# A quarter of the gate and up contraction by Strassen's seven block products, in a two-layer decoder trunk on one core

## The chip, the cores and the metric

The kernel runs on one core of one Trainium2 chip. The metric is the device time of one execution in microseconds (us); before the change it is 2117.68 us, the median of three runs (2116.63 to 2117.85 us).

## The reference

Two layers act on 256 tokens of width 2048. The first mixes by a diagonal state space (S5) and a gated projection, the second by causal attention. Each then has a SwiGLU of inner width 5632, which holds most of the arithmetic:

```python
D_MODEL = 2048; SEQ = 256; D_FF = 5632

def swiglu(u, w_gate, w_up, w_down):
    return (jax.nn.silu(u @ w_gate) * (u @ w_up)) @ w_down

for i in range(DEPTH):                       # DEPTH = 2
    ...                                      # mixer of layer i
    u = rmsnorm(h, g_ffn[i])
    h = h + swiglu(u, w_gate[i], w_up[i], w_down[i])
return rmsnorm(h, g_final)
```

Everything is float32 at the interface.

## The kernel before, in words

Every weight matrix is cut into tiles of 512 rows by 512 columns (1 MB). Such a tile is one job. All 344 jobs stand in one list, and `run_stream` goes through it: matmuls of job i, then the preparation of job i+2 (`split_upto`), then whatever functions were pended behind job i. The order on each engine is the order in which these calls are written; no scheduler changes it.

Preparing a job: SyncE loads the tile into `raw` (three buffers); ScalarE rounds it to `hi` (L98) and VectorE forms `lo = raw - hi` (L99), each in two halves of 128x1024. `hi` and `lo` have two buffers each, so job i+2 can be rounded when job i's matmuls have let go. In the first seven jobs GpSimd forms `lo`. The activations are split in the same way, so a product is three matmuls: hi by hi, lo by hi, hi by lo (`mm3`, L108 to L110). A job of the kind used here is 4 blocks of 128 rows x 2 token halves x 3 = 24 matmuls with 512 columns.

In the SwiGLU the inner width is 11 chunks of 512 columns: 6 in the first half of the stage, 5 in the second, each half followed by its part of the down projection. A chunk is 4 gate jobs and 4 up jobs (the input width 2048 is 4 tiles of 512 rows). Each job adds into two PSUM banks, one per token half. Chunks alternate between the four `acc` banks and the `x` and `tr` banks. ScalarE takes silu of the gate banks (L686), VectorE multiplies by the up banks (L693), and two jobs into the next chunk TensorE transposes the product row by row (L701), ScalarE and VectorE splitting it into `g` (L704, L705).

The activations `u_f` are transposed from `h` by `hT_blocks`: four blocks of 128 features per call of `u_chunk`, TensorE (L141), ScalarE (L145), VectorE (L146). For the first SwiGLU these calls stand among the last jobs of the gated projection (there GpSimd adds bias and residual, L597 and L611, and VectorE multiplies, L609); for the second among the last jobs of the output projection of the attention (`w_o`).

Of the kernel before, what the change touches and what calls it, by code (L numbers as in the profile page):

```python
# [30 lines left out]
def trunk_kernel(ctx: ExitStack, tc: tile.TileContext, par, x_tok, x_grp, b_st, g_st, c_st, cst, gvec,  # L31
# [57 lines left out]
    def split_upto(n):
        while st["split"] < min(n, len(jobs)):  # L90
            i = st["split"]
            load_upto(i + 3)
# [8 lines left out]

    def mm3(psums, opnd, kb0, j, first, last, kbs=range(4), halves=range(2)):
        for kb in kbs:
            for a in halves:
# [2 lines left out]
                pr = psums[a]
                pe.matmul(pr, oh, j.hi[:, kb], start=first and kb == 0, stop=False)  # L108
                pe.matmul(pr, ol, j.hi[:, kb], start=False, stop=False)  # L109
                pe.matmul(pr, oh, j.lo[:, kb], start=False, stop=last and kb == 3)  # L110
# [24 lines left out]
    def hT_blocks(blocks, dst, g, base=0):  # L135
        for b0 in range(0, len(blocks), 2):
# [5 lines left out]
            for bb in range(2):  # L142
# [510 lines left out]
    def g_at(l, hf, kb):  # L653
        n, b = divmod(kb, 8)
        if (l, hf, n) not in G:
            G[l, hf, n] = big.tile([128, 2, 8, L], F32R, name=f"g{l}{hf}{n}", tag="ABC"[n])
# [527 lines left out]
```

## Time and profile before

| | |
|---|---|
| median of three runs | 2117.68 us |
| the profiled execution | 2113.61 us, span 2111.8 us |
| TensorE matmuls busy | 2082.5 us, 99% |
| VectorE busy | 1135.2 us, 54% |
| ScalarE busy | 905.6 us, 43% |
| GpSimd busy | 150.1 us, 7% |
| read from HBM | 370 MB, 176 GB/s over the span |

The span is what the trace covers; the profiled execution's own time is 1.8 us more. Busy time of matmuls counts overlapping ones once. In the tables of groups, the busy time and mean of a matmul include the time in which the next one already runs.

### The profile page before, as it was taken

To read this page: it belongs to the slowest core of one execution; us is meant where nothing else is said; L and a number is where in the kernel's file an instruction comes from. 1 tells how busy PE (TensorE), PEld (TensorE's weight loads), DVE (VectorE), ACT (ScalarE), POOL (GpSimd) and SP (SyncE) were. 2 spreads that over 40 slices of the span, in tenths; PEclk is the share of its full clock that TensorE was granted. 3 is DMA by queue.
4 is the path that set the end of the run, shared out by engine and by line. 5 is a ranking of instruction groups with operands and counts; after the bars stand their busy time and mean duration, and the time that the engine had idled before them with its cause. 6 is when DMAs were issued, how large, how long until landed. Compare 5 with 4: busy or idle time off the path is not lost.

```text
span 2111.8 us, 27975 instructions
## 1 busy us (share of the span) xinstructions
PE 2082.5 (99%) x11712; PEld 1754.9 (83%) x11712; DVE 1135.2 (54%) x1661; ACT 905.6 (43%) x1161; POOL 150.1 (7%) x105
## 2 busy tenths in 40 slices
PE   7999999999999999999999999999999999999998
PEld 6778788888888888889999998888888888888886
DVE  8984854444444445455555455554444544445454
ACT  6344544434334344444444444454444333443443
POOL 7741400000000000000000000000000000000000
PEclk9999999999999999999999999999999999999999
DMA  3035555555555555555545544555555555555554
GB/s 140 25 126 157 197 190 188 197 183 197 182 197 199 181 197 180 198 180 180 180 160 180 172 167 160 181 193 184 185 194 193 186 199 190 189 192 186 195 194 149
DMA packets 54046, 376.14 MB, mean 178 GB/s; under 512 B 6432, under 2 KB 6944, under 8 KB 9120
## 3 DMA queue, kind: packets, MB, share of 16 engines
q1 hardware_dynamic: 53920, 374.36, 51.5%
q8 instruction: 91, 1.49, 0.3%
q14 instruction: 35, 0.29, 0.0%
HBM read 370.14 MB, written 2.10 MB: 176 GB/s over the span
## 4 chain that ended last, share of the span: by engine, by line
PE 95%; DVE 3%; ACT 1%; issue 1%; DMA 0%; SPq 0%; ACTq 0%; POOLq 0%; POOL 0%
PE acc L109 18%; PE acc L110 18%; PE acc L108 18%; PE x L110 4%; PE x L108 4%; PE x L109 4%; PE tr L109 4%; PE tr L108 4%; PE tr L110 4%; PE acc L793 3%; PE acc L792 3%; PE acc L791 3%; PE x L464 1%; PE tr L141 1%; PE acc L273 1%
## 5 line engine op out<-in xcount | busy, mean ns | idle before, releaser
L99 DVE TENSOR_TENSOR lo<-raw,hi 128x1024 fp32r<-128x1024 f32 x674 | 805.9, 1237 | 674.5 <-ACT hi L98 674.4
L98 ACT ACTIVATE hi<-raw 128x1024 fp32r<-128x1024 f32 x688 | 690.4, 1052 | 715.4 <-PE acc L109 413.3
L108 PE MATMUL acc<-hi,g 128*128 128x512 f32 x704 | 274.9, 390 | 0.0
L110 PE MATMUL acc<-lo,g 128*128 128x512 f32 x704 | 274.0, 389 | 0.0
L109 PE MATMUL acc<-hi,g 128*128 128x512 f32 x704 | 274.0, 389 | 0.0
L108 PE MATMUL acc<-hi,u_f 128*128 128x512 f32 x640 | 251.1, 392 | 1.1 <-ACT hi L98 1.0
L110 PE MATMUL acc<-lo,u_f 128*128 128x512 f32 x640 | 249.5, 390 | 1.1 <-DVE lo L99 1.1
L109 PE MATMUL acc<-hi,u_f 128*128 128x512 f32 x640 | 249.3, 390 | 0.0
L110 PEld LDWEIGHTS acc<-lo,g 128*128 128x128 f32 x704 | 132.2, 188 | 27.6
L109 PEld LDWEIGHTS acc<-hi,g 128*128 128x128 f32 x704 | 132.2, 188 | 27.1
L108 PEld LDWEIGHTS acc<-hi,g 128*128 128x128 f32 x704 | 132.2, 188 | 27.1
L108 PE MATMUL x<-hi,u_f 128*128 128x512 f32 x384 | 151.3, 394 | 0.0
L110 PE MATMUL x<-lo,u_f 128*128 128x512 f32 x384 | 149.7, 390 | 0.0
L109 PE MATMUL x<-hi,u_f 128*128 128x512 f32 x384 | 149.5, 389 | 0.0
L108 PE MATMUL tr<-hi,u_f 128*128 128x512 f32 x384 | 149.4, 389 | 0.0
L109 PE MATMUL tr<-hi,u_f 128*128 128x512 f32 x384 | 149.4, 389 | 0.0
L110 PE MATMUL tr<-lo,u_f 128*128 128x512 f32 x384 | 149.4, 389 | 0.0
L110 PEld LDWEIGHTS acc<-lo,u_f 128*128 128x128 f32 x640 | 120.1, 188 | 26.9 <-DVE lo L99 1.9
L108 PEld LDWEIGHTS acc<-hi,u_f 128*128 128x128 f32 x640 | 120.2, 188 | 26.4 <-ACT hi L98 1.9
L109 PEld LDWEIGHTS acc<-hi,u_f 128*128 128x128 f32 x640 | 120.2, 188 | 24.8 <-DVE u_f L146 0.3
L110 PEld LDWEIGHTS x<-lo,u_f 128*128 128x128 f32 x384 | 72.1, 188 | 15.2
L108 PEld LDWEIGHTS tr<-hi,u_f 128*128 128x128 f32 x384 | 72.1, 188 | 15.0
(238 smaller groups left out, 2865.1 us busy)
## 6 DMA issues: line engine op xcount, KB each, us to landing
raw<-w_gate SPq DMA_DIRECT2D x88, 1024.0 KB, 4.8
raw<-w_up SPq DMA_DIRECT2D x88, 1024.0 KB, 4.8
raw<-w_down SPq DMA_DIRECT2D x88, 1024.0 KB, 4.8
raw<-w_kv SPq DMA_DIRECT2D x32, 1024.0 KB, 4.8
raw<-w_glu SPq DMA_DIRECT2D x16, 1024.0 KB, 4.9
raw<-w_q SPq DMA_DIRECT2D x16, 1024.0 KB, 4.8
raw<-w_o SPq DMA_DIRECT2D x16, 1024.0 KB, 4.8
h<-x_tok SPq DMA_DIRECT2D x2, 1024.0 KB, 7.8
```

What stands on the lines that cost most here:

```text
L98: act.activation(j.hi[:, s], j.raw[:, s], AF.Copy)
L99: (pool if i < NPRE else dve).tensor_tensor(j.lo[:, s], j.raw[:, s], j.hi[:, s], op=OP.subtract)
L108: pe.matmul(pr, oh, j.hi[:, kb], start=first and kb == 0, stop=False)
L109: pe.matmul(pr, ol, j.hi[:, kb], start=False, stop=False)
L110: pe.matmul(pr, oh, j.lo[:, kb], start=False, stop=last and kb == 3)
L141: pe.transpose(tr[:, bb, a], h[:, a, 128 * b:128 * b + 128], ident)
L273: pe.matmul(wbk[:, 0:w], ident, cs[:, 0:w], start=True, stop=True)
L464: pe.matmul(yb[64 * g2:64 * g2 + 64, g], H[q][r, ri, gl + g2].rearrange("p k c -> p (k c)"), Z[r, :, ri, 2 * (8 * o + g) + b], start=ri == ...
L791: pe.matmul(p, j.hi[:, kb, s], u[:, 0], start=first and kb == 0 and n % 2 == 0, stop=False)
L792: pe.matmul(p, j.hi[:, kb, s], u[:, 1], start=False, stop=False)
L793: pe.matmul(p, j.lo[:, kb, s], u[:, 0], start=False, stop=last and kb == 3 and n % 2 == 1)
```

## The change

For 10 of the 11 chunks of each layer (all but chunk 0) the first tile of 512 rows of gate and up is no longer two jobs of 24 matmuls. With the activations as a 2x2 matrix of blocks (token half x 256 rows) and the weights as another (256 rows x gate or up), the product is formed with seven block products instead of eight (`s_add`, `mm1`: 6 matmuls each). The weight sums are four additions of 128x1024 on VectorE per chunk (`S_T1` to `S_T4`, L769); the two tiles are loaded into buffers of their own (`s_load`); products 1 to 7 are jobs of one half unit each, rounded like the others. The activation sums are made once per layer in `s_combine`, which takes the place of the first `hT_blocks`. Some products stand in two or more of the four results. They are added by reading the PSUM bank between products into a row (`s_evac`) and correcting the results with it after the last job. The other three tiles of gate and up (`X` jobs) add into the same banks, partly between the products. `hi` and `lo` become two fixed buffers used half by half; the pool of rows goes from 5 to 9 buffers; the transposed result of chunk c goes to banks of chunk c itself.

```diff
-    rows = ctx.enter_context(tc.tile_pool(name="rows", bufs=5))
+    rows = ctx.enter_context(tc.tile_pool(name="rows", bufs=9))
...
+            if j.make is not None:
+                j.make()
+            for p in range(units(j)):
+                raw = j.raw[:, 2 * p:2 * p + 2] if j.part is None else j.part()
+                u = st["unit"]
+                st["unit"] += 1
+                hi, lo = [t[:, 2 * (u % 2):2 * (u % 2) + 2] for t in parts[u // 2 % 2]]
+                act.activation(hi, raw, AF.Copy)
+                (pool if i < NPRE else dve).tensor_tensor(lo, raw, hi, op=OP.subtract)
...
+    def split_ahead(i):
+        split_upto(i + 2)
+        n = units(jobs[i + 1]) if i + 1 < len(jobs) else 3
+        k = i + 2
+        while k < len(jobs) and n + units(jobs[k]) <= 3:
+            n += units(jobs[k])
+            k += 1
+        split_upto(k)
...
+    def mm1(pr, opnd, j, first, join):
+        for kb in range(2):
+            oh, ol = opnd(0, kb), opnd(1, kb)
+            pe.matmul(pr, oh, j.hi[kb], start=first and kb == 0, stop=False, skip_group_check=join)
+            pe.matmul(pr, ol, j.hi[kb], start=False, stop=False, skip_group_check=join)
+            pe.matmul(pr, oh, j.lo[kb], start=False, stop=first and kb == 1, skip_group_check=join)
...
+    def s_combine(un, g):
...
+        for b in range(2):
...
+            for bb in range(2):
+                k = b + 2 * bb
+                x = X[:, bb].rearrange("p a t -> p (a t)")
+                act.activation(X[:, bb], tr[:, bb], AF.Copy, scale=g[:, k:k + 1])
+                act.activation(uT[un][:, 0, k], x, AF.Copy)
+                dve.tensor_tensor(uT[un][:, 1, k], x, uT[un][:, 0, k], op=OP.subtract)
+            dve.tensor_tensor(V[:, 2], X[:, 0, 1], X[:, 0, 0], op=OP.subtract)
+            dve.tensor_tensor(V[:, 0], X[:, 0, 1], X[:, 1, 1], op=OP.subtract)
+            dve.tensor_tensor(V[:, 1], X[:, 1, 1], V[:, 2], op=OP.subtract)
+            dve.tensor_tensor(V[:, 3], X[:, 1, 0], V[:, 1], op=OP.subtract)
+            act.activation(SC["c"][:, 0, :, b], V, AF.Copy)
+            dve.tensor_tensor(SC["c"][:, 1, :, b], V, SC["c"][:, 0, :, b], op=OP.subtract)
...
+            for t, w in (("F", wu), ("E", wg)):
+                nc.sync.dma_start(T[t], w[4 * c].rearrange("p (k n) -> p k n", k=4))
...
+            if n == 0:
+                gr[c, 0] = row()
+                act.activation(P(), acc["gate"][0], AF.Copy)
+            if n == 1:
+                T["u"] = row()
+                tt(T["u"], acc["up"][0], P(), OP.subtract)
+            if n == 2:
+                tt(T["u"], acc["up"][1], T["u"], OP.add)
+            if n == 4:
+                gr[c, 1] = row()
+                tt(v(), acc["up"][0], P(), OP.subtract)
+            if n == 9:
+                T["s"] = row()
+                act.activation(T["s"], acc["gate"][0], AF.Silu, scale=r[:, 0:1])
+                tt(T["u"], acc["gate"][1], T["u"], OP.subtract)
+                act.activation(T["u"], T["u"], AF.Silu, scale=r[:, 1:2])
+            if n == 12:
+                tt(P(), acc["up"][0], P(), OP.subtract)
+                tt(P(), P(), T["s"], OP.mult)
+                tt(v(), acc["up"][1], v(), OP.add)
+                tt(v(), v(), T["u"], OP.mult)
+                gu_end()
...
+                    pend.append((j0 - 5, s_load(l, c, wg, wu)))
+                    pend.append((j0 - 3, S_T1))
+                    pend.append((j0 - 2, S_T2))
+                    pend.append((j0 - 2, S_T3))
+                    for i in (1, 6, 7):
+                        s_add(i, un, own)
+                    X("gate", wg, 1)
+                    s_add(5, un, own)
+                    X("gate", wg, 2)
+                    for i in (2, 3, 4):
+                        s_add(i, un, own)
+                    X("gate", wg, 3)
+                    for kg in (1, 2, 3):
+                        X("up", wu, kg)
+                    for n in (0, 1, 2, 4, 9, 12):
+                        pend.append((j0 + n, s_evac(n, c, r)))
```

So a changed chunk is 13 jobs: products 1, 6, 7 (P1, P6, P7), gate tile 1 (X1), P5, gate tile 2 (X2), P2, P3, P4, gate tile 3 (X3), up tiles 1 to 3 (U1 to U3).

How instructions now stand, at three places. First TensorE at the start of chunk 1, where before the first job of a chunk goes to both gate banks (`x`) in turn, three matmuls each; before:

```order
L108 MATMUL x_3145<-hi_3173,u_f_2665 128x512
L109 MATMUL x_3145<-hi_3173,u_f_2665 128x512
L110 MATMUL x_3145<-lo_3174,u_f_2665 128x512
L108 MATMUL x_3146<-hi_3173,u_f_2665 128x512
L109 MATMUL x_3146<-hi_3173,u_f_2665 128x512
L110 MATMUL x_3146<-lo_3174,u_f_2665 128x512
```

and of the change, the end of P1, the start of P6, the start of P7, and the transposes of chunk 0 behind it (`sc` holds the activation sums):

```order
L144 MATMUL x_3126<-lo_1488,u_f_2641 128x512
L142 MATMUL tr_3138<-hi_1487,sc_u_f_2642 128x512
L143 MATMUL tr_3138<-hi_1487,sc_u_f_2642 128x512
L144 MATMUL tr_3138<-lo_1488,sc_u_f_2642 128x512
...
L142 MATMUL tr_3139<-hi_1495,sc_u_f_2642 128x512
...
L849 MATMUL acc_137_3162<-cs,row_3031 128x128 x4
```

A product stays in one bank for six matmuls and takes a new `hi` and `lo` half; over the whole program TensorE has 120 rows fewer (9231 for 9351).

Second, ScalarE at the start of a chunk. Before, the gate banks of the old chunk have long been read, and roundings of whole tiles follow one another up to the copy of the transposed rows:

```order
L98 ACTIVATE hi_3734<-raw_3666 128x1024 x2
L98 ACTIVATE hi_3768<-raw_3698 128x1024 x2
L704 ACTIVATE g_3779<-acc_149_3774 128x4x128
L98 ACTIVATE hi_3808<-raw_3732 128x1024 x2
L704 ACTIVATE g_3779<-acc_150_3814 128x4x128
```

Of the change, at the start of chunk 3 (`st` and `su` are weight sums, the L808 row is the reading of P1 from its bank, `raw_3675` is X1):

```order
L111 ACTIVATE hi_1495<-st_3_3553 128x1024
L111 ACTIVATE hi_1487<-su_3_3552 128x1024
L808 ACTIVATE row_3693<-x_3685 128x512
L111 ACTIVATE hi_1487<-raw_3675 128x1024
L111 ACTIVATE hi_1495<-raw_3675 128x1024
L111 ACTIVATE hi_1495<-st_3_3553 128x1024
L852 ACTIVATE g_3724<-acc_157_3719 128x4x128
```

The rounding of X1 now stands behind a reading that waits for P1's last matmul.

Third, VectorE near the end of the gated projection, where `u_f` of the first SwiGLU is begun. Before:

```order
L609 TENSOR_TENSOR row_2615<-row_2615,zk 128x8x32 x2
L609 TENSOR_TENSOR row_2616<-row_2616,zk 128x8x32 x2
L146 SCALAR_TENSOR_TENSOR u_f_2665<-tr_2666,gv,u_f_2665 128x256 x2
L146 SCALAR_TENSOR_TENSOR u_f_2665<-tr_2675,gv,u_f_2665 128x256 x2
L99 TENSOR_TENSOR lo_2711<-raw_2603,hi_2710 128x1024 x2
```

Of the change (the six rows of `X_u_f_2663` that follow, alike, are left out):

```order
L672 TENSOR_TENSOR row_2594<-row_2594,zk 128x8x32 x2
L201 TENSOR_TENSOR u_f_2641<-X_u_f_2644,u_f_2641 128x256 x2
L202 TENSOR_TENSOR V_u_f_2645<-X_u_f_2644 128x128
L203 TENSOR_TENSOR V_u_f_2645<-X_u_f_2644 128x128
L204 TENSOR_TENSOR V_u_f_2645<-X_u_f_2644,V_u_f_2645 128x128
L205 TENSOR_TENSOR V_u_f_2645<-X_u_f_2644,V_u_f_2645 128x128
L207 TENSOR_TENSOR sc_u_f_2642<-V_u_f_2645,sc_u_f_2642 128x4x128
...
L112 TENSOR_TENSOR lo_1488<-raw_2583,hi_1487 128x1024 x2
```

The rounding of the second-last job of the projection stands behind 14 operations of VectorE where there were 4, and on ScalarE, in the same place, behind 10 where there were 4.

## Rows read from the trace of the kernel before

**Rows 1.** The page: busy time and share of each engine.

```profile
PE 2082.5 (99%) x11712; PEld 1754.9 (83%) x11712; DVE 1135.2 (54%) x1661; ACT 905.6 (43%) x1161; POOL 150.1 (7%) x105
```

**Rows 2.** Windows: busy of each engine, TensorE's clock, DMA share, GB/s.

```profile
1600.00:1700.00 100.00, 100.00 (x450) 82.84 (x449) 48.81 (x46) 39.28 (x42) 0.00 (x0) 1.00 0.55 189
222.00:265.00 43.00, 40.81 (x190) 32.29 (x188) 35.71 (x45) 23.83 (x42) 16.96 (x12) 1.00 0.50 175
```

**Rows 3.** Timeline of TensorE, 1640 to 1653 us: start, duration.

```profile
1640.87 0.39 PE L108 MATMUL acc<-hi,g 128*128 128x512 f32 x1
...
1650.85 0.39 PE L110 MATMUL acc<-lo,g 128*128 128x512 f32 x1
...
1651.76 0.60 PE L701 MATMUL x<-cs,row 128*128 128x128 f32 x4
...
1652.43 0.39 PE L109 MATMUL acc<-hi,g 128*128 128x512 f32 x1
```

**Rows 4.** Groups by shape, 1400 to 2000 us: busy, mean ns | idle before.

```profile
L99 DVE TENSOR_TENSOR lo<-raw,hi 128x1024 fp32r<-128x1024 f32 x217 | 256.2, 1222 | 252.1 <-ACT hi L98 252.1
L693 DVE TENSOR_TENSOR row<-tr,row 128x512 f32<-128x512 f32 x12 | 7.7, 681 | 0.0
...
L98 ACT ACTIVATE hi<-raw 128x1024 fp32r<-128x1024 f32 x217 | 218.1, 1052 | 284.4 <-PE acc L109 164.3 <-PE tr L109 75.4 <-PE x L109 44.6
L704 ACT ACTIVATE g<-acc 128x512 fp32r<-128x512 f32 x10 | 6.0, 598 | 37.6 <-PE acc L701 37.6
```

**Rows 5.** Groups by shape, whole run: smaller operations of both engines.

```profile
L236 DVE TENSOR_TENSOR gam<-gam,T 128x256 f32<-128x256 f32 x1 | 0.4, 419 | 0.0
L224 DVE TENSOR_TENSOR gam<-gam 128x64 f32<-128x64 f32 x1 | 0.2, 218 | 0.0
...
L133 ACT ACTIVATE jk<-h 128x512 f32<-128x512 f32 x30 | 18.8, 626 | 25.0 <-DVE h L727 15.0 <-DVE h L722 8.3 <-POOL h L611 1.6
L499 ACT ACTIVATE zT<-tr 128x256 fp32r<-128x256 f32 x16 | 4.8, 388 | 7.1 <-PE tr L494 7.1
```

**Rows 6.** Timeline: ScalarE's start behind TensorE, VectorE's behind ScalarE.

```profile
1640.85 2.01 ACT L98 ACTIVATE hi<-raw 128x1024 fp32r<-128x1024 f32 x2 [3.43 <-PE tr L109]
...
1641.94 2.36 DVE L99 TENSOR_TENSOR lo<-raw,hi 128x1024 fp32r<-128x1024 f32 x2 [3.08 <-ACT hi L98]
```

**Rows 7.** Timelines of four engines at the end of the gated projection.

```profile
225.32 0.47 ACT L145 ACTIVATE u_f<-tr,gv 128x256 fp32r<-128x256 f32 x1 [1.37 <-PE tr L141]
...
229.03 2.00 ACT L98 ACTIVATE hi<-raw 128x1024 fp32r<-128x1024 f32 x2
...
220.31 4.06 DVE L99 TENSOR_TENSOR lo<-raw,hi 128x1024 fp32r<-128x1024 f32 x2
...
230.11 2.36 DVE L99 TENSOR_TENSOR lo<-raw,hi 128x1024 fp32r<-128x1024 f32 x2 [0.47 <-ACT hi L98]
...
219.76 3.53 POOL L597 TENSOR_TENSOR row<-row,row 128x512 f32<-128x512 f32 x2 [1.76 <-DVE row L596]
...
226.95 1.29 POOL L611 TENSOR_TENSOR h<-h,row 128x512 f32<-128x512 f32 x1 [0.43 <-DVE row L609]
...
231.03 0.39 PE L108 MATMUL acc<-hi,zT 128*128 128x512 f32 x1
...
231.48 0.41 PE L110 MATMUL acc<-lo,zT 128*128 128x512 f32 x1
...
243.52 0.50 PE L108 MATMUL acc<-hi,u_f 128*128 128x512 f32 x1 [0.51 <-ACT hi L98]
```

**Rows 8.** Timelines at the attention's output projection, ScalarE and TensorE.

```profile
1333.92 0.47 ACT L145 ACTIVATE u_f<-tr,gv 128x256 fp32r<-128x256 f32 x1 [0.63 <-PE tr L141]
...
1336.73 2.00 ACT L98 ACTIVATE hi<-raw 128x1024 fp32r<-128x1024 f32 x2
...
1340.43 0.48 PE L108 MATMUL acc<-hi,o 128*128 128x512 f32 x1
```

**Rows 9.** The page, DMA issues: KB each, us from issue to landing.

```profile
raw<-w_gate SPq DMA_DIRECT2D x88, 1024.0 KB, 4.8
```

More of the change, by code (lines that the diff above doesn't have):

```diff
@@ L106, in mm3 @@
                 ol = opnd(1, kb0 + kb, a)
[L107 to L110, printed above, removed]
+                pr, jn = psums[a], a in joins
+                pe.matmul(pr, oh, j.hi[kb], start=first and kb == 0 and not jn, stop=False, skip_group_check=jn)
+                pe.matmul(pr, ol, j.hi[kb], start=False, stop=False, skip_group_check=jn)
+                pe.matmul(pr, oh, j.lo[kb], start=False, stop=last and kb == 3 and not jn, skip_group_check=jn)
+    def mm1(pr, opnd, j, first, join):
[4 more added lines that the diff above has]
+            pe.matmul(pr, oh, j.lo[kb], start=False, stop=first and kb == 1, skip_group_check=join)
     def run_stream(i0, i1):
@@ L578, in f @@
                 u_tile(name)
-            hT_blocks(range(4 * c, 4 * c + 4), uT[name], gv[:, gs])
+            if c == 0 and name != "u_kv":
+                s_combine(name, gv[:, gs])
+            else:
+                hT_blocks(range(4 * c, 4 * c + 4), uT[name], gv[:, gs])
         pend.append((j, f))
@@ L655, in g_at @@
         if (l, hf, n) not in G:
[L656 removed]
+            G[l, hf, n] = big.tile([128, 2, 8, L], F32R, name=f"g{l}{hf}{n}", tag=("ABC", "BCD")[l][n])
         return G[l, hf, n], b
@@ L669, in gu_acc, with gu_end, gu_job @@
             new_acc(nm)
+            CT[nm] = last_tags()
         else:
             acc[nm] = [bank("x" if nm == "gate" else "tr") for _ in range(2)]
-    def gu_job(nm, un, own, kg):
+            CT[nm] = ["x" if nm == "gate" else "tr"] * 2
+    def gu_end():
+        NT[:] = [CT["gate"][0], CT["up"][1]]
+    def gu_job(nm, un, own, kg, first, last, joins=None):
         o = opnd1(lambda: uT[un])
         def f(j):
-            if kg == 0:
+            if joins is None and first:
                 gu_acc(nm, own)
-            mm3(acc[nm], o, 4 * kg, j, kg == 0, kg == 3)
+            mm3(acc[nm], o, 4 * kg, j, first, last, joins=joins or ())
+        return f
@@ L694, in up_evac, with g_rows @@
         return f
-    def g_rows(l, hf, c, own, a):
+    def g_rows(l, hf, c, src, a):
         def f():
-            t = sil[c][a]
-            tr = bank(own if own else "x").rearrange("p (b t) -> p b t", b=4)
+            t = src()
+            tr = bank(NT[a]).rearrange("p (b t) -> p b t", b=4)
             for b in range(4):
```

107 lines of the change are left out of this document (83 added, 24 removed).

## Prediction

> **What bounds the kernel now.** I read the page first. TensorE is busy 99% of the span, VectorE 54%, ScalarE 43% [rows 1]. A busy TensorE need not be at its peak, so the windows come next: in a stretch inside the SwiGLU TensorE is busy 100.00 of 100 us at granted clock 1.00 (its upper level, 2.4 GHz), VectorE 48.8, ScalarE 39.3, GpSimd 0, DMA 0.55 [rows 2]. The timeline of that stretch shows matmuls at a fixed pace: from 1640.87 to 1650.85 us there are 44 intervals, 0.2268 us each [rows 3]. The 0.39 us of one matmul overlaps the next; the price of a matmul with 512 columns is 0.2268 us. Other engines wait there: VectorE for ScalarE (252 us in 600), ScalarE for TensorE (284 us) [rows 4]. So in the SwiGLU a matmul less is time less, as long as VectorE and ScalarE stay ahead.
>
> One place is different. At the end of the gated projection VectorE is busy 35.7 of 43 us, and TensorE waits: the first gate matmul starts at 243.52 behind the rounding by ScalarE [rows 2, 7]. There the chain through VectorE and ScalarE sets the end, and the change puts work into that chain.
>
> **What is removed.** Per changed chunk 48 matmuls become 7 x 6 = 42. 10 chunks in 2 layers: 120 matmuls, the 120 rows that TensorE has fewer. 120 x 0.2268 = 27.2 us [rows 3]. The Trainium skill (TensorE: Matmul & The Clock Gate, section "Wait — 56ns, not 53.3ns?") gives columns / 2.4 GHz + 2.5 ns from start to start, 215.7 ns at 512 columns; by it the term would be 25.9 us. The row has 226.8 ns, and I use the row.
>
> **What a changed chunk asks of VectorE and ScalarE.** TensorE's time: 186 matmuls x 0.2268 = 42.2 us, and two groups of transposes, each 0.45 us (1651.76 to 1652.43 less one interval) [rows 3]: 43.1 us. VectorE: 19 roundings for 16 and 4 weight sums, which have the shape and both operands in SBUF like L99: 23 x 1.22 = 28.1; 8 operations of 512 columns in `s_evac` and 2 of `g_rows` at 0.68: 6.8 [rows 4]. Sum 34.9 of 43.1 us (before: 16 x 1.22 + 4 x 0.68 = 22.2 of 44.4). ScalarE: 19 x 1.05 + some 5 x 0.65 = 23 us. All lie under TensorE as totals, so what counts is where TensorE waits for one late item. I followed the orders of a chunk with these durations and 0.04 us between engines (1640.85 + 1.05 to 1641.94) [rows 6].
>
> The tightest place is X1 at the start of a chunk. On ScalarE the reading of P1 (0.60, as L704) stands ahead of X1's rounding [rows 4]. P1's last matmul ends 0.39 - 0.23 = 0.16 us into P6. Then 0.04 + 0.60, + 1.05 for `hi`, + 0.04 + 1.22 for `lo`, + 0.05 until TensorE: 3.2 us. TensorE gets to X1's third matmul, the first that needs `lo`, after P6 and P7 (12 x 0.2268 = 2.72), one group of transposes (0.45) and two matmuls (0.45): 3.6 us. Slack 0.45 us. VectorE is free by then: its four operations on the old chunk end 0.16 + 4 x 0.68 = 2.9 us after that chunk's last matmul, and `hi` of X1 comes 1.36 (P1) + 0.16 + 0.64 + 1.05 = 3.2 us after it. The other places have more. P4, behind the sum `S_T4`, which stands behind the reading of P5: from P5's end VectorE still has P2's `lo` (1.7 with its `hi`), then 0.68 + 1.22 + 1.22, then ScalarE 1.05 and `lo` 1.22, 7.1 us in all; TensorE has X2, P2, P3 and two matmuls, 8.6 us. At U2, VectorE waits for X3's end to read a gate bank, with U2's rounding queued behind; U2 is needed one job (5.44 us) later. Nothing here waits, so I cost the products, sums and readings at nothing; the cover is 0.45 us per chunk at the least, and each 0.1 us beyond it would cost 20 x 0.1 = 2 us.
>
> Readings between products also hold back TensorE's next write to the bank: P1's bank is written again by X1, 3.2 us later, when the reading has taken 0.8; P6's by P5, P5's by P3, each with a job of 5.44 us between. No wait.
>
> **Transfers.** Bytes are the same; two tiles go to buffers of their own. They are issued when P3 and `S_T4` let go, some 6 us before X3, and are needed by `S_T1` about two jobs later, 15 us after issue, against 4.8 us to land one and a DMA share of 0.55 [rows 2, 9]. In SyncE's queue U3's tile stands behind them; it waits for X3's rounding anyway. No cost.
>
> **What is added once per layer: `s_combine`.** On ScalarE one of its two halves is: scale, round, scale, round (0.47 and 0.39 twice, 1.7 us, as in [rows 5, 7]), then VectorE's second `lo` (0.42) and four sums of 128 columns, between the 0.22 of 64 and the 0.42 of 256 columns, with two dependent pairs (1.2 us together), then the rounding of 512 columns (0.63) [rows 5]. That is 4.0 us, and the second half stands behind the first on ScalarE: 8.0 us until ScalarE can round the next weight tile.
>
> First SwiGLU: before, ScalarE starts at 225.32 and rounds the next tile at 229.03, 3.7 us later [rows 7]. Now 8.0: 4.3 us late. That tile's job starts at 231.03, and its third matmul came a trace late already (0.41 us for 0.39, at 231.48) [rows 7]: no slack. The chain from there to 243.52 is VectorE's and ScalarE's, where TensorE waits even now, so the delay isn't made up: + 4.3 us.
>
> Second SwiGLU: before, 1333.92 to 1336.73 [rows 8]. Now the rounding starts at 1341.9, `hi` is there at 1343.0, `lo` at 1344.3. The job started at 1340.43 [rows 8] and would need `lo` 0.54 us later: + 3.3 us. The next `u_chunk` and rounding then come late too, by 0.3 us beyond the delayed job: + 3.6 us. Bounds for both layers: if the sums go at 0.22 us and the operations overlap at the seams, a half is 3.5 us and the cost 3.3 + 2.6 = 5.9 us; if the sums take 0.42 us each, a half is 4.5 us and the cost 9.9. I take 7.9, near the middle, since 128 columns lie between the two rows.
>
> **Sum.** - 27.2 + 7.9 = - 19.3 us. The profiled execution is 2113.6 us (span 2111.8 + 1.8), which would become 2094.3. The median of the three runs lies 4.1 us above it; the same difference gives 2117.7 - 19.3 = **2098.4 us**, 0.9% less.
>
> **The rivals.**
> 1. `s_combine` is hidden: TensorE has work queued, or the later stalls before the SwiGLU shrink by what is lost ahead of them. Then 27.2 less at most 3: 2090.5 to 2093.5. Against it: TensorE waits there already [rows 7].
> 2. The start of a chunk waits. If reading P1 or rounding X1 comes 0.5 us beyond the slack, 20 x 0.5 = 10 us: 2108. For it: 0.45 us is thin, and ScalarE has a waiting instruction ahead of X1. Against it: the rows of the long operations vary little.
> 3. GpSimd slows `s_combine`. While GpSimd adds (219.76 to 223.3) VectorE's two roundings take 4.06 us instead of 2.36 [rows 7]; the replaced L146 reads PSUM and was not slowed. GpSimd's next addition, 226.95 for 1.29 us, lies on the first operations of `s_combine`, which read two operands from SBUF: up to 1.3 us more, 2099.7. The Trainium skill (SBUF — State Buffer, section "Who interferes with whom") says of two such operations that the second blocks until the first ends; by that rule the whole 1.29 us is added.
> 4. The other side: VectorE becomes the bound in the chunks. With d for an operation of 1024 columns its work is 23 d + 6.8; it fills 43.1 us at d = 1.58 us, and at 1.62 us (1 us over, in 20 chunks) the gain of 19.3 is gone; with 1.7 us, 20 x 2.8 = 56 us: 2154. For it: 2.03 us is what L99 takes beside GpSimd [rows 7]. Against it: GpSimd has no instruction in the SwiGLU [rows 2], and 1.22 is the mean of 217 [rows 4].
> 5. The seven products aren't cheaper: six matmuls in a row into one bank, or a wait for a half at each, at 0.26 us instead of 0.2268 for 840 matmuls, + 28 us: no change. Against it: three in a row into one bank show no longer interval [rows 3].
>
> **How the numbers follow.** Forecast 0.55 (2094 to 2103 with the bounds of `s_combine` and some tenths per chunk); rival 1 0.12; rival 2 0.15; rival 3 0.10; rival 4 0.04; rival 5 0.04. Range 2091 to 2107: rival 1 nearly whole, the forecast, rival 3, half of rival 2. A measurement of this kernel tells 0.2% (4.2 us) from no change. Faster: all but rivals 4 and 5 and the far end of 2: 0.90; same 0.05; slower 0.05.
>
> **What would show it.** Right: TensorE's matmuls of 512 columns 120 fewer at the same 0.227 us; in the 20 chunks no row of TensorE that waits for X1's `lo` or `hi`; the first gate matmul not at 243.5 but about 4 us later, and gaps of about 3 us in all at the 11th of the 16 jobs of `w_o`; VectorE at some 80% in the chunks. Wrong: gaps in front of X1 or P4 in every chunk; a mean of L112 over 1.3 us there; a longer interval inside a product; or no delay at `s_combine`.

## The result: 2097.6 us, 1.0% faster, and the profile after

The changed kernel takes 2097.62 us (median of 4 runs, 2094.18 to 2098.23) against 2117.76 us of the kernel before on the same chip (4 runs, 2116.63 to 2118.51): a ratio of 0.9902, 95% interval 0.9885 to 0.9919. The forecast was 2098.4 us. The execution that was profiled took 2097.13 us, with a span of 2095.3 us (before: 2113.6 and 2111.8).

Line numbers below are those of the changed kernel: `mm3` is L135 to L137 and `mm1` L142 to L144 (third matmul, the one that needs `lo`: L137, L144), the rounding of a weight tile is L111 (`hi`) and L112 (`lo`), `s_combine` L195 to L207, the plain path for the activations L175 to L180, a weight sum L769, the reading of P1 L808.

First the page's line of busy times; it answers to [rows 1].

```profile
PE 2061.8 (98%) x11592; PEld 1736.3 (83%) x11592; DVE 1387.9 (66%) x1941; ACT 1000.5 (48%) x1253; POOL 149.9 (7%) x105
```

TensorE has 120 matmuls fewer, VectorE 280 instructions more. TensorE still fills the span. The windows show what the busy share hides (window, its length, busy time of PE, PEld, DVE, ACT and POOL with counts, TensorE's clock, DMA share, GB/s): one stretch in the chunks, and the two places where TensorE had waited for `s_combine`.

```profile
236.00:240.00 4.00, 2.97 (x7) 2.12 (x8) 3.75 (x6) 4.00 (x8) 0.47 (x1) 0.65 0.16 25
1336.00:1340.00 4.00, 3.62 (x9) 2.91 (x10) 2.91 (x6) 1.91 (x6) 0.00 (x0) 0.57 0.40 100
1500.00:1600.00 100.00, 100.00 (x454) 82.85 (x453) 78.64 (x80) 51.72 (x58) 0.00 (x0) 1.00 0.51 180
```

In the chunks TensorE is busy 100.00 of 100 us at clock 1.00, with VectorE at 78.6 where it was at 48.8 [rows 2]. At the other two places the clock was down to 0.65 and 0.57, which no window of before shows. The groups of 1400 to 2000 us answer to [rows 4]: one rounding on VectorE still takes 1223 ns, so more work on that engine did not make it slower.

```profile
L112 DVE TENSOR_TENSOR lo<-raw,hi 128x1024 fp32r<-128x1024 f32 x182 | 217.7, 1223 | 97.0 <-ACT hi L111 95.0
L111 ACT ACTIVATE hi<-raw 128x1024 fp32r<-128x1024 f32 x183 | 189.9, 1056 | 113.2 <-PE acc L136 78.5 <-PE tr L136 19.0 <-PE x L136 5.4
```

TensorE's list of waits over the whole run names the two places, and of 300 to 1250 us and 1385 to 2080 us it has no entry at all: no chunk waits (us in total, times, longest).

```profile
PE acc L135 <- ACT hi L111: 5.8, 3, 3.7
...
PE acc L137 <- DVE lo L112: 1.6, 3, 0.5
```

The account is made with instructions that stand at the same point of both programs. First in the trace of before (start, duration), then after: a matmul behind the transposes that feed `uT` (gated projection, then attention output projection), and the first matmul of the second SwiGLU.

```profile
225.79 0.39 PE L109 MATMUL acc<-hi,zT 128*128 128x512 f32 x1
...
1334.39 0.39 PE L109 MATMUL acc<-hi,o 128*128 128x512 f32 x1
...
1373.18 0.39 PE L108 MATMUL acc<-hi,u_f 128*128 128x512 f32 x1
```

```profile
227.45 0.39 PE L136 MATMUL acc<-hi,zT 128*128 128x512 f32 x1
...
1327.11 0.39 PE L136 MATMUL acc<-hi,o 128*128 128x512 f32 x1
...
1370.26 0.39 PE L135 MATMUL acc<-hi,u_f 128*128 128x512 f32 x1
```

- Up to the first marker: 227.45 - 225.79 = + 1.66 us. Nothing there was changed: the first matmul of the state-space part (L397, before L337) comes at 25.13 instead of 23.44 us. Over the profiled executions of all kernels here it lies between 23.3 and 27.7 us, and one kernel (the filled waits, below) has it at 23.90 in one execution and at 26.30 in another. It is the spread between executions.
- From the first marker to the matmul that follows the last wait in chunk 0 (265.37 us before, 271.71 after): 44.26 us for 39.58, + 4.68.
- From the second marker to the second SwiGLU: 43.15 us (1370.26 - 1327.11) for 38.79, + 4.36.
- The rest: from the end of chunk 0's waits to the second marker 1055.40 us for 1069.02, from the second SwiGLU's first matmul to the end of the span 725.04 for 738.62, - 13.62 and - 13.58 us, where 60 matmuls fewer in each layer make 60 x 0.2268 = 13.61.

The sum, 1.66 + 4.68 + 4.36 - 27.20 = - 16.5 us, is the difference of the spans. So 27.2 us were gained, and about 9 us were lost at the two calls of `s_combine`.

How they are lost can be read from ScalarE at the first of them.

```profile
226.98 0.47 ACT L199 ACTIVATE X_u_f<-tr,gv 128x256 f32<-128x256 f32 x1 [1.37 <-PE tr L195]
...
231.20 0.63 ACT L206 ACTIVATE sc_u_f<-V_u_f 128x512 fp32r<-128x512 f32 x1 [2.48 <-DVE V_u_f L205]
231.74 0.46 ACT L199 ACTIVATE X_u_f<-tr,gv 128x256 f32<-128x256 f32 x1
...
234.88 0.63 ACT L206 ACTIVATE sc_u_f<-V_u_f 128x512 fp32r<-128x512 f32 x1 [1.42 <-DVE V_u_f L205]
235.41 1.99 ACT L111 ACTIVATE hi<-raw 128x1024 fp32r<-128x1024 f32 x2
```

From the first scaling to the rounding of the next weight tile it is 8.43 us, before 3.71 [rows 7]. ScalarE stands still for 2.48 and 1.42 us of it: the rounding of the first block's sums (L206) waits for VectorE, and the second block's scaling (L199) stands behind it in ScalarE's queue although its transposes are done. In the second layer the same stretch is 7.38 us (before 2.81 [rows 8]). VectorE's row says why the first layer's is longer:

```profile
228.38 1.84 DVE L201 TENSOR_TENSOR u_f<-X_u_f,u_f 128x256 fp32r<-128x256 f32 x2
...
232.68 0.43 DVE L201 TENSOR_TENSOR u_f<-X_u_f,u_f 128x256 fp32r<-128x256 f32 x1
```

Two operations take 1.84 us where one takes 0.43 a little later, and it is the second of them that is long (beside it GpSimd):

```profile
228.75 1.48 DVE L201 TENSOR_TENSOR u_f<-X_u_f,u_f 128x256 fp32r<-128x256 f32 x1
...
228.61 1.34 POOL L674 TENSOR_TENSOR h<-h,row 128x512 f32<-128x512 f32 x1 [0.43 <-DVE row L672]
```

GpSimd adds from 228.61 to 229.95 us. And TensorE, after its wait:

```profile
236.50 0.50 PE L135 MATMUL acc<-hi,zT 128*128 128x512 f32 x1 [3.66 <-ACT hi L111]
236.84 0.39 PE L136 MATMUL acc<-hi,zT 128*128 128x512 f32 x1
237.76 0.79 PE L137 MATMUL acc<-lo,zT 128*128 128x512 f32 x1 [0.53 <-DVE lo L112]
238.35 0.63 PE L135 MATMUL acc<-hi,zT 128*128 128x512 f32 x1
238.78 0.63 PE L136 MATMUL acc<-hi,zT 128*128 128x512 f32 x1
...
240.49 0.47 PE L137 MATMUL acc<-lo,zT 128*128 128x512 f32 x1
```

From 238.35 us on the matmuls start 0.43 us apart (238.78 - 238.35), not 0.227: TensorE's lower clock, 1.2 GHz, by the granted 0.65 of that window.

### The profile page after: what moved, and what is told of

It reads as the page before. It is cut to its first block, busy times and chain, and to the rows that moved or that the text cites. A ratio compares the mean times of both kernels' runs of the same rounds, so it can differ in the third digit from the quotient of the medians.

```text
span 2095.3 us, 28782 instructions
## 1 busy us (share of the span) xinstructions
PE 2061.8 (98%) x11592; PEld 1736.3 (83%) x11592; DVE 1387.9 (66%) x1941; ACT 1000.5 (48%) x1253; POOL 149.9 (7%) x105
## 4 chain that ended last, share of the span: by engine, by line
PE 92%; DVE 5%; ACT 1%; issue 1%; DMA 1%; SPq 1%; ACTq 0%; POOLq 0%; POOL 0%; DVEq 0%
PE acc L137 16%; PE acc L135 16%; PE acc L136 16%; PE x L137 3%; PE x L135 3%; PE x L136 3%; PE tr L135 3%; PE tr L137 3%; PE tr L136 3%; PE acc L961 3%; PE acc L960 3%; PE acc L959 3%; PE x L524 1%; PE acc L144 1%; PE acc L142 1%; PE acc L143 1%
## 5 line engine op out<-in xcount | busy, mean ns | idle before, releaser
L112 DVE TENSOR_TENSOR lo<-raw,hi 128x1024 fp32r<-128x1024 f32 x594 | 721.1, 1241 | 341.9 <-ACT hi L111 337.2
L111 ACT ACTIVATE hi<-raw 128x1024 fp32r<-128x1024 f32 x608 | 627.2, 1055 | 346.9 <-PE acc L136 248.6
L135 PE MATMUL acc<-hi,g 128*128 128x512 f32 x704 | 274.9, 390 | 0.0
L137 PE MATMUL acc<-lo,g 128*128 128x512 f32 x704 | 274.0, 389 | 0.0
L135 PE MATMUL acc<-hi,u_f 128*128 128x512 f32 x512 | 200.5, 392 | 0.6 <-ACT hi L111 0.5
L137 PE MATMUL acc<-lo,u_f 128*128 128x512 f32 x512 | 199.6, 390 | 0.5 <-DVE lo L112 0.5
L136 PE MATMUL acc<-hi,u_f 128*128 128x512 f32 x512 | 199.4, 389 | 0.0
L137 PEld LDWEIGHTS acc<-lo,g 128*128 128x128 f32 x704 | 132.2, 188 | 27.6
L135 PEld LDWEIGHTS acc<-hi,g 128*128 128x128 f32 x704 | 132.2, 188 | 27.0
L111 ACT ACTIVATE hi<-st 128x1024 fp32r<-128x1024 f32 x60 | 63.4, 1056 | 115.2 <-DVE st L769 115.2
L137 PEld LDWEIGHTS acc<-lo,u_f 128*128 128x128 f32 x512 | 96.1, 188 | 21.3 <-DVE lo L112 1.3
L135 PEld LDWEIGHTS acc<-hi,u_f 128*128 128x128 f32 x512 | 96.1, 188 | 20.8 <-ACT hi L111 0.9
L135 PE MATMUL x<-hi,u_f 128*128 128x512 f32 x288 | 113.0, 392 | 0.0
L136 PEld LDWEIGHTS acc<-hi,u_f 128*128 128x128 f32 x512 | 96.2, 188 | 20.0 <-DVE u_f L180 0.3
L137 PE MATMUL x<-lo,u_f 128*128 128x512 f32 x288 | 112.2, 390 | 0.0
L136 PE MATMUL x<-hi,u_f 128*128 128x512 f32 x288 | 112.1, 389 | 0.0
L135 PE MATMUL tr<-hi,u_f 128*128 128x512 f32 x288 | 112.0, 389 | 0.0
L136 PE MATMUL tr<-hi,u_f 128*128 128x512 f32 x288 | 112.0, 389 | 0.0
L137 PE MATMUL tr<-lo,u_f 128*128 128x512 f32 x288 | 112.0, 389 | 0.0
L112 DVE TENSOR_TENSOR lo<-st,hi 128x1024 fp32r<-128x1024 f32 x60 | 73.4, 1223 | 25.7 <-ACT hi L111 24.1
```

What stands on the lines that cost most here:

```text
L111: act.activation(hi, raw, AF.Copy)
L112: (pool if i < NPRE else dve).tensor_tensor(lo, raw, hi, op=OP.subtract)
L135: pe.matmul(pr, oh, j.hi[kb], start=first and kb == 0 and not jn, stop=False, skip_group_check=jn)
L136: pe.matmul(pr, ol, j.hi[kb], start=False, stop=False, skip_group_check=jn)
L137: pe.matmul(pr, oh, j.lo[kb], start=False, stop=last and kb == 3 and not jn, skip_group_check=jn)
```

## The experiments

The theory: the chunks lose nothing, and all of the 9 us stands at `s_combine`. Rivals: the loss is spread over the chunks (rival 2 of the prediction), VectorE is the bound or close to it (rival 4), GpSimd is to blame (rival 3). All times are medians; kernels of one group shared a chip and the runs of the kernel before, 2115.5 to 2115.7 us there.

**The sums, moved to where nothing waits.** `u_chunk` takes the plain path for all blocks again; the sums follow in chunk 0, from `uT`'s two parts:

```diff
-            if c == 0 and name != "u_kv":
-                s_combine(name, gv[:, gs])
-            else:
-                hT_blocks(range(4 * c, 4 * c + 4), uT[name], gv[:, gs])
+            hT_blocks(range(4 * c, 4 * c + 4), uT[name], gv[:, gs])
...
+        def sums():
...
+            dve.tensor_tensor(x, uT[un][:, 0, 0:4].bitcast(F32), uT[un][:, 1, 0:4].bitcast(F32), op=OP.add)
+            X = x.rearrange("p (k b) (a t) -> p k b a t", b=2, a=2)
+            dve.tensor_tensor(V[:, 2], X[:, 0, :, 1], X[:, 0, :, 0], op=OP.subtract)
...
+                    for n, f in enumerate(s_late(un)):
+                        pend.append((j0 + 2 + n, f))
```

Expected: 

> The activations go to their layout by the path of the kernel before (uT straight out of PSUM), and the sums of them are formed from uT's two parts during chunk 0 of each SwiGLU, where nothing waits for them until chunk 1's P6. Theory (the whole loss of some 9 us against 120 x 0.2268 = 27.2 us stands at the two s_combine places, +4.7 and +4.4 us): about 9 us less than the changed kernel, 2088.5 us (2087 to 2090.5), and no wait of TensorE for L111 around 230 and 1333 us. Rival (the loss is spread over the chunks, or stands at the start of each): no more than 2 us less, 2095.5 to 2098. Rival (the sums cost the same wherever they stand, since VectorE is nearly full): 2096 to 2098, with waits in chunk 0.

Measured: 2088.36 us, ratio to before 0.9871 (0.9858 to 0.9885); span 2085.1 us. ScalarE in that kernel, at the gated projection:

```profile
225.22 0.47 ACT L179 ACTIVATE u_f<-tr,gv 128x256 fp32r<-128x256 f32 x1 [1.37 <-PE tr L175]
...
228.93 2.00 ACT L111 ACTIVATE hi<-raw 128x1024 fp32r<-128x1024 f32 x2
```

3.71 us, as before the change. First place (the stretch from the first marker, above): 39.55 us against 39.58 before the change; second place 38.79 against 38.79. The late sums cost 0.5 us once, in the first layer's chunk 0, where VectorE does them ahead of a tile that is due (TensorE waits 0.30 us for L112 at 271.19). The theory holds, both rivals fall: the sums at another place are nearly free. Their form changed with their place (fewer and wider operations, which start from `uT`'s parts), and this run does not part the two. This kernel beats both others, by 27 us the kernel before and by 7 to 9 us the changed one (8 to 10 us by the spans of the profiled executions).

**`s_combine` without the products.** All chunks by eight products, the sums formed and not read:

```diff
-                if c == 0:
+                if True:
                     for nm, w in (("gate", wg), ("up", wu)):
```

Expected: 

> All 11 chunks of both SwiGLUs are computed by eight products, as before the change; s_combine stays, and its sums are read by nobody. Theory (s_combine alone loses some 9 us and the chunks lose nothing): the kernel before + 7.5 to 9.5 us, 2125 to 2127 us (what the sums cost at the end of a projection, without any gain). Rival (the loss is in the chunks): the time of the kernel before within 1.5 us, 2116.5 to 2119.

Measured: 2124.34 us, ratio 1.0043 (1.0029 to 1.0057), that is 9.1 us slower than before (6 to 12). The time is below the 2125 to 2127 us expected, since the kernel before ran at 2115.47 us on this chip; the difference is the one expected. In its trace the first place costs 4.68 us and the second 4.30, and TensorE waits nowhere in the SwiGLUs. With the experiment before, both halves of the account are there alone: - 27.2 from the products, + 9 from the sums' place.

**The order inside `s_combine`.** The same instructions; first the scalings and roundings of both blocks, then the eight sums, then the roundings of the sums:

```diff
+        XV = []
         for b in range(2):
...
+            XV.append((X, V))
+        for b in range(2):
+            X, V = XV[b]
             dve.tensor_tensor(V[:, 2], X[:, 0, 1], X[:, 0, 0], op=OP.subtract)
...
+        for b in range(2):
+            V = XV[b][1]
             act.activation(SC["c"][:, 0, :, b], V, AF.Copy)
```

Expected: 

> s_combine issues the same instructions in another order: first the copies and roundings of both blocks, then the eight sums, then the two roundings of the sums (in the changed kernel ScalarE stands still 1.42 us twice, 2.48 and 1.42 us in layer 0, because the rounding L206 of the first block's sums is ahead of the second block's copies in its queue). Theory (half of the loss is that order, the rest the work itself): from the first L199 to the next L111 6.3 to 6.7 us in layer 1 (7.38 now) and 6.5 to 7.8 us in layer 0 (8.43 now), 1 to 2 us less in all, 2095.5 to 2096.6 us. Rival (the work counts, the order does not): 2097 to 2098 us with 7.2 to 7.5 us there.

Measured: 2093.31 us (2092.08 to 2094.76), ratio 0.9894 (0.9880 to 0.9907), 2.8 us below the changed kernel on that chip (2096.14, below). ScalarE in the second layer:

```profile
1326.72 0.47 ACT L200 ACTIVATE X_u_f<-tr,gv 128x256 f32<-128x256 f32 x1 [1.75 <-PE tr L196]
...
1331.51 0.63 ACT L212 ACTIVATE sc_u_f<-V_u_f 128x512 fp32r<-128x512 f32 x1 [1.42 <-DVE V_u_f L209]
1332.44 0.63 ACT L212 ACTIVATE sc_u_f<-V_u_f 128x512 fp32r<-128x512 f32 x1 [0.30 <-DVE V_u_f L209]
1332.97 1.99 ACT L111 ACTIVATE hi<-raw 128x1024 fp32r<-128x1024 f32 x2
```

6.25 us for 7.38, and 6.37 for 8.43 in the first layer: the order counts. The time is below what was expected (2095.5 to 2096.6 us). More was gained in the first layer, 2.1 us on ScalarE: GpSimd still holds up one VectorE operation there (1.48 us at 230.97), but ScalarE goes on with the second block meanwhile. And no matmul ran at half speed at either place of this execution; whether the shorter waits (1.6 and 0.6 us) or chance kept the clock up, one execution doesn't tell.

**GpSimd beside `s_combine`.** First try: GpSimd's addition of the gated chunk 1 to `h` was put one job later in the program.

```diff
-            hs = h[:, a, 512 * c:512 * c + 512]
-            pool.tensor_tensor(hs, hs, t, op=OP.add)
+            if c != 1:
+                glu_add(c, a)
...
     def glu_sq(c):
+        if c == 1:
+            for a in range(2):
+                glu_add(c, a)
         sq_chunk(c)
```

Expected: 

> GpSimd adds the gated chunk 1 to h one job later, so that no GpSimd instruction runs beside s_combine's first operations on VectorE in layer 0 (in the changed kernel POOL L674 runs 228.61 to 229.95 us, and two VectorE operations L201 take 1.84 us there against 0.43 each in layer 1). Theory (GpSimd holds VectorE up): the first two L201 take 0.40 to 0.45 us each, and from the first L199 to the next L111 it is 7.3 to 7.5 us in layer 0 (8.43 now); at the first SwiGLU, where other waits take up part of it, 0 to 1 us less; 2096.5 to 2098 us. Rival (those two wait for something else, their operand or each other): 1.84 us and 8.4 us as before.

Measured: 2098.48 us, and the edit moved nothing: the additions still start at 229.07 and 230.84 us, as soon as VectorE's products are there, beside the two L201 (1.85 us). GpSimd's queue held nothing ahead of them. So VectorE was given the two additions, one job later:

```diff
     def glu_add(c, a):
         hs = h[:, a, 512 * c:512 * c + 512]
-        pool.tensor_tensor(hs, hs, gt[c][a], op=OP.add)
+        (dve if c == 1 else pool).tensor_tensor(hs, hs, gt[c][a], op=OP.add)
```

Expected: 

> The run before left GpSimd's additions at the same time (they start as soon as their operands are there, wherever they stand in the program). Now VectorE adds the gated chunk 1 to h itself, one job later, behind s_combine's operations; GpSimd has nothing to do beside the first two L201 of layer 0. Theory (GpSimd holds VectorE up): those two take 0.40 to 0.45 us each, and from the first L199 to the next L111 it is 7.3 to 7.5 us in layer 0 (8.43 now); 0 to 1 us less up to the first SwiGLU, less what the two additions cost VectorE (2 x 0.6 us); 2094.5 to 2097.5 us. Rival (the two wait for something else): 1.84 us together and 8.4 us as before.

Measured: 2097.35 us. VectorE:

```profile
228.58 0.42 DVE L201 TENSOR_TENSOR u_f<-X_u_f,u_f 128x256 fp32r<-128x256 f32 x1 [0.57 <-ACT u_f L200]
229.39 0.42 DVE L201 TENSOR_TENSOR u_f<-X_u_f,u_f 128x256 fp32r<-128x256 f32 x1 [0.39 <-ACT u_f L200]
...
238.35 1.29 DVE L678 TENSOR_TENSOR h<-h,row 128x512 f32<-128x512 f32 x2
```

0.42 us each, and 7.38 us instead of 8.43 on ScalarE: GpSimd had held VectorE up by 1.05 us. But the time is no less (first place + 5.0 us): in its trace the two additions now stand on VectorE (1.29 us) ahead of the gating sums and the next rounding, in the same chain. What the 1.05 us is worth without that was not tried.

**The clock.** Multiplications of constants into an unused bank during the two waits:

```diff
+    def fill_wait(j, n):
+        jobs[j].pre.append(lambda: warm(n, cs[:, 0:256]))
+
+    fill_wait(len(jobs) - 2, 8)
     ffn(0, "u_f0", w_gate0, w_up0, w_down0, sml[:, 1], down0_evac)
...
+    fill_wait(jo0 + 10, 4)
```

Expected: 

> During the two waits for s_combine TensorE multiplies constants into an unused bank: 8 such matmuls of 256 columns ahead of the gated projection's last job but one, 4 ahead of the third job of the attention's output projection's second half. Theory (the half-speed matmuls of 0.42 to 0.43 us after the waits, seven and eight of them, come from the clock that falls while TensorE waits): granted clock 1.00 in both places, no interval of 0.43 us there, and 1.3 to 1.6 us less by the second place (first matmul of the second SwiGLU to that of the first); at the first place 0 to 1.5 us less. In all 2094.5 to 2096.5 us. Rival (the intervals come from late operands or from the order of the queue): the same intervals and 2097 to 2099 us.

Expected of its second execution: 

> The kernel that fills both waits with multiplications of constants, once more. Over eight executions of kernels with the same waits unfilled, 6 to 14 matmuls behind the first wait ran at half speed in all eight, and 6 or 7 behind the second in five of eight. Theory (the clock falls while TensorE waits): none here at either place, granted clock 1.00. Rival (chance): half-speed matmuls behind the first wait.

Measured: 2096.43 us (2095.59 to 2097.21), and 2096.75 us. Windows of the first:

```profile
236.00:240.00 4.00, 3.28 (x14) 2.09 (x13) 3.75 (x5) 4.00 (x8) 0.24 (x1) 1.00 0.01 2
...
1336.00:1340.00 4.00, 3.47 (x16) 2.87 (x16) 2.92 (x6) 1.91 (x6) 0.00 (x0) 1.00 0.35 92
```

Clock 1.00 and no half-speed matmul, in both executions at both places. The price of the fall in these rows: the first place costs 4.67 and 4.70 us with the fill, 4.68 without, so nothing here, because TensorE waits again right behind it; the second place 3.04 and 3.01 us with the fill, 4.36 without. 1.3 us in all, too little to be told in the total (2097.62 and 2096.14 us for the kernel without the fill).

**The changed kernel once more**, with no edit.

Expected: 

> The changed kernel once more, beside the two others on one chip: 2095 to 2098.5 us, with 8.43 and 7.38 us from the first L199 to the next L111, and half-speed matmuls after both waits.

Measured: 2096.14 us (2094.93 to 2097.64), ratio 0.9907 (0.9894 to 0.9921). 8.44 and 7.39 us on ScalarE; behind the first wait 14 half-speed matmuls (place + 5.15 us), behind the second none (+ 3.03 us). So the expectation was half wrong: with the same wait the clock falls in one execution and not in another. That makes the unfilled second place of this execution equal to the filled ones.

The two places side by side, all from the timelines (ScalarE: first scaling to next L111; cost: against 39.58 and 38.79 us of before):

| kernel | ScalarE, 1st | cost | half-speed | ScalarE, 2nd | cost | half-speed |
|---|---|---|---|---|---|---|
| before | 3.71 | 0 | 0 | 2.81 | 0 | 0 |
| changed | 8.43 | 4.68 | 6 | 7.38 | 4.36 | 7 |
| changed, again | 8.44 | 5.15 | 14 | 7.39 | 3.03 | 0 |
| waits filled | 8.43 | 4.67 | 0 | 7.38 | 3.04 | 0 |
| sums last | 6.37 | 2.61 | 0 | 6.25 | 1.93 | 0 |
| sums late | 3.71 | 0, and 0.5 behind it | 0 | 2.82 | 0 | 0 |

The first place costs what ScalarE comes late (8.43 - 3.71 = 4.72; 6.37 - 3.71 = 2.66), the second 1.5 us less than that (7.38 - 2.81 = 4.57 for 3.04; 6.25 - 2.81 = 3.44 for 1.93).

**How much room X1 has.** ScalarE reads P1 again, to the same place, ahead of X1's rounding (shown for two readings; three in the other kernel):

```diff
             if n == 0:
                 gr[c, 0] = row()
-                act.activation(P(), acc["gate"][0], AF.Copy)
+                for _ in range(2):
+                    act.activation(P(), acc["gate"][0], AF.Copy)
```

Expected of two readings: 

> ScalarE reads P1 twice in each chunk (20 chunks), the second time to the same place; each reading holds ScalarE for about 0.5 us from start to next start (L808 1503.40 to L111 1503.89). The rounding of X1's tile stands behind it. Theory (X1 has a slack of some 0.45 to 0.58 us before TensorE waits): X1's first wait of 0 to 0.15 us per chunk, so 0 to 3 us more, 2097 to 2101 us. Rival (there is a hidden slack of more than 1 us, as for the other jobs): no change. Rival (X1 is already at the edge): 20 x 0.5 = 10 us more, 2107 us.

Expected of three: 

> The same with two further readings of P1, so 1.0 to 1.2 us more of ScalarE ahead of X1's rounding. Theory (a slack of 0.45 to 0.58 us): 0.45 to 0.7 us of waiting in each of 20 chunks, 9 to 14 us more than the changed kernel, 2106 to 2112 us, and more if the clock falls behind each wait. Rival (more than 1.2 us of slack): 2097 to 2099 us.

Measured: 2101.06 us (ratio 0.9929, 0.9915 to 0.9944) and 2112.99 us (0.9988, 0.9978 to 0.9997). TensorE at X1 of one chunk of the second layer, with two readings, then with three:

```profile
1508.77 0.40 PE L136 MATMUL x<-hi,u_f 128*128 128x512 f32 x1
1509.06 0.50 PE L137 MATMUL x<-lo,u_f 128*128 128x512 f32 x1
1509.40 0.39 PE L135 MATMUL x<-hi,u_f 128*128 128x512 f32 x1
```

```profile
1515.52 0.39 PE L136 MATMUL x<-hi,u_f 128*128 128x512 f32 x1
1516.45 0.50 PE L137 MATMUL x<-lo,u_f 128*128 128x512 f32 x1 [0.54 <-DVE lo L112]
1516.78 0.40 PE L135 MATMUL x<-hi,u_f 128*128 128x512 f32 x1
```

From one chunk's X1 to the next it is 43.11 us in the changed kernel, 43.29 with two readings, 43.91 with three (1515.52 to 1559.43). One reading more holds ScalarE for 0.64 us (from the reading's start to L111 1.13 us for 0.49) and costs 0.18 us; the next costs 0.62. VectorE and TensorE in the changed kernel show what the first had for cover:

```profile
1504.97 2.36 DVE L112 TENSOR_TENSOR lo<-raw,hi 128x1024 fp32r<-128x1024 f32 x2 [0.86 <-ACT hi L111]
...
1506.82 0.40 PE L137 MATMUL x<-lo,u_f 128*128 128x512 f32 x1
```

The first half of X1's `lo` is done at 1504.97 + 1.22 = 1506.19 us, TensorE can use it 0.06 us later (with three readings 1515.17 + 1.22 = 1516.39, used at 1516.45) and gets to it at 1506.82: a slack of 0.57 us. A reading of 0.64 us leaves a wait of 0.07 us, and a matmul that waits at all holds up the next by 0.11 us more (1509.06 to 1509.40 is 0.34 us, not 0.227); together the 0.18. Beyond the slack every 0.1 us costs 2 us. By these rows the two kernels cost 20 chunks x 0.18 = 3.6 and x 0.80 = 16 us more. The first time was at the upper end of what the theory gave (2097 to 2101 us), the second 1.0 us above it (2106 to 2112); the rivals (no slack, or more than 1 us of it) fall.

**How much room VectorE has.** Sums of 128x1024 that are read by nobody, four per chunk (shown), then eight (behind jobs 3, 4, 5, 6, 8, 9, 10 and 11 of the chunk, counted from 0):

```diff
-        SC["c"] = big.tile([128, 2, 4, 2, 128], F32R, name=f"sc_{un}", tag="DA"[un == "u_f1"])
+        SC["c"] = big.tile([128, 4, 4, 2, 128], F32R, name=f"sc_{un}", tag="DA"[un == "u_f1"])
...
+                    for n in (5, 8, 10, 11):
+                        pend.append((j0 + n, lambda: dve.tensor_tensor(SC["c"][:, 2], uT[un][:, 0, 0:4].bitcast(F32),
+                                                                       uT[un][:, 1, 0:4].bitcast(F32), op=OP.add)))
```

Expected of four: 

> VectorE forms four further sums of 128x1024 in each chunk (after X2, P4, U1 and U2; read by nobody), 4 x 1.14 to 1.22 us. Theory (VectorE is busy 34 to 35 of 43.1 us of a chunk and bounds nothing): 38.5 to 39.8 of 43.1 us, no more than 2 us in all, 2097 to 2100 us. Rival (VectorE is the bound of the chunks already, the gaps in its row being waits of its own chain): 20 x 4.7 = 94 us more, 2190 us.

Expected of eight: 

> Eight such sums in each chunk (after X1, P5, X2, P2, P4, X3, U1 and U2). Theory: 34 to 35 + 8 x 1.14 to 1.22 = 43.1 to 44.7 us of VectorE against 43.1 of TensorE, VectorE meets the bound: 0 to 1.6 us in each of 20 chunks, and some waits where sums stand ahead of a tile that is due, so 2100 to 2135 us with TensorE waiting for L112. Rival (VectorE is the bound already): 20 x 9.5 = 190 us more. Rival (much room is left): 2097 to 2099 us.

Measured: 2096.61 us with four, no change, and no wait of TensorE between 1400 and 1700 us; 2165.52 us with eight (ratio 1.0232, 1.0217 to 1.0248). The four rule out VectorE as the bound. The eight missed what the theory expected (2100 to 2135), and the rows say why. VectorE, then TensorE at X3:

```profile
1515.17 1.23 DVE L112 TENSOR_TENSOR lo<-st,hi 128x1024 fp32r<-128x1024 f32 x1 [1.21 <-ACT hi L111]
1516.32 2.48 DVE L909 TENSOR_TENSOR sc_u_f<-u_f 128x1024 fp32r<-128x1024 f32 x2
1518.71 2.35 DVE L112 TENSOR_TENSOR lo<-raw,hi 128x1024 fp32r<-128x1024 f32 x2
```

```profile
1519.98 0.50 PE L137 MATMUL acc<-lo,u_f 128*128 128x512 f32 x1 [1.87 <-DVE lo L112]
```

Two of the sums stand ahead of X3's `lo` at the place where VectorE has the least time (behind `S_T4` and P4), and TensorE waits 1.4 to 1.9 us for it in each of the 20 chunks (1.87 here), while VectorE has idle time elsewhere (41.8 to 43.4 us busy of a period of 47). In 12 of the 20 chunks the clock falls behind that wait (granted 0.96 in 1504 to 1551 us). A chunk takes 45.7 us where it holds and 47.3 where it falls, for 43.1. VectorE's work alone would have lengthened a chunk of 43.1 us by 0.3 us at most. So most of the loss is the order again, and the clock behind it; eight sums at better places were not tried.

## Why the prediction was right

- **The matmuls.** 120 x 0.2268 = 27.2 us was the term, 13.6 + 13.6 us the measured one. Six matmuls in a row into one bank start 0.227 us apart (L142 to L144), so rival 5 is out.
- **The chunks cost nothing.** Shown by the waits (none), by the sums moved late (all of the loss gone), and by the readings of P1: X1 has a slack, 0.57 us where 0.45 was worked out. The forecast let a reading hold ScalarE for its whole 0.60 us; the next operation starts after 0.49. What a wait costs beyond its length (0.11 us) was in no term. That 0.46 us of the first extra reading were free (0.64 - 0.18), next to the 0.45 forecast, is therefore luck. VectorE at 78.6% was forecast as some 80% and bounds nothing: rivals 2 and 4 are out.
- **Transfers.** No wait for a tile in the chunks; right.
- **`s_combine`.** Forecast + 4.3 and + 3.6, together 7.9 us; measured 4.7 and 4.4, together 9.0, inside its bounds of 5.9 to 9.9. The mechanism was right and the size was made of other parts. A half of it takes 3.7 us, not 4.0 (1326.64 to 1330.34 for the first half in the second layer, 7.38 for both, not 8.0), since ScalarE stands still for 1.43 us where 0.42 + 1.2 was put, and goes on 0.54 us after L206's start, not 0.63. Alone that gives 3.67 + 3.04 = 6.7 us, 1.2 less than forecast. GpSimd adds 1.05 us in the first layer: rival 3, true as a mechanism, below the 1.3 that it gave as the most, and priced outside the sum. The clock adds 1.3 us in the second layer in the profiled execution. That term was in no part of the prediction. The first gate matmul stands 5.4 us later behind the first marker (23.15 us for 17.73; about 4 was forecast), 4.7 us with the waits filled: the 0.7 us between is the clock at the first place, and shorter waits behind it give that back. So the sum came out within its bounds by a half that was put too long and two costs that were left out of it: that 7.9 lies near 9.0 is in part luck.
- **The total.** The profiled execution should have come to 2094.3 us and took 2097.1: 1.1 us from `s_combine`, 1.7 us from the start of that execution. The forecast for the median added 4.1 us, the distance of the median before from its profiled run; after, the two lie 0.5 us apart. So the 0.8 us between forecast and median is partly luck, the range is not.
- **Rival 1**, that `s_combine` is hidden, fell: at the first place the waits behind it gave back nothing of ScalarE's delay (4.72 late, 4.68 lost). The sums can be hidden, but in chunk 0, not where they stood.

## What to carry to other kernels

Work that is added once is cheap or dear by its place more than by its amount: the sums cost 9 us where ScalarE and VectorE set the end and 0.5 us when formed 40 us later, where TensorE had work queued; look for such a place before the operation count is trimmed. Two engines that hand blocks to and fro should not have a block's last step ahead of the next block's first one in an in-order queue (the other order won 1.1 us of ScalarE's time in the second layer and 2.1 us in the first). Before adding to an engine that looks free in total, find the one item in the period with the least slack; its few tenths of a microsecond are what fits there for nothing, and what goes beyond them is paid in every period.

## What the runs showed of the hardware that was not expected

**TensorE's clock fell at waits of 1.7 to 3.7 us in an otherwise busy stretch.** Nine profiled executions (the changed kernel twice, and all its variants but the late sums, the sums last and the filled waits) had both waits unfilled. Behind the first, 6 to 14 matmuls ran at or near half speed in all nine; behind the second, 6 or 7 in six of nine and none in three. Filled, none at four places. The fall need not lie in the wait itself: in the rows shown above TensorE resumes with an interval of 0.34 us (236.50 to 236.84), as behind any wait, and the slow ones begin at 237.76; with two readings of P1 the first one is slow already (0.59 us at 236.31). The Trainium skill (TensorE: Matmul & The Clock Gate, section "Part 1: The HAM clock gate (the "warmup" mystery)") says that the number of slow matmuls at the start of a kernel varies from run to run of the same kernel. Behind a wait it does so here too, with 6 and 14 behind the same wait of the same kernel. What the fall costs depends on what follows: 1.1 to 1.3 us where TensorE is the bound again, at most 0.5 us where it has to wait anyway.

**A matmul behind a wait costs 0.11 us beyond the wait**: 0.34 us instead of 0.227 to the next start (1516.45 to 1516.78), also where the clock stays at 1.00.

**GpSimd held up VectorE by 1.0 us** (1.84 us for two of 256 columns with both operands in SBUF, 0.42 each once GpSimd was idle; the first, issued 0.23 us before GpSimd's addition, took 0.41 and the second 1.48). The Trainium skill (SBUF — State Buffer, section "Who interferes with whom") calls the port pair that the two engines share an exclusive lock; the rows agree: the second operation ended at 230.23 us, 0.28 us after GpSimd's addition.
